# Gated layer's second projection: both column pairs by seven block products, with its token sums made in the last gated head's second group

## The chip, the cores and the metric

The kernel runs on one core of one Trainium2 chip. The metric is the device time of one execution in microseconds; the runs of the kernel before took 1377.15, 1377.93 and 1378.95 us. A core has five engines with queues of their own: TensorE (PE; its weight loads are listed as PEld), VectorE (DVE), ScalarE (ACT), GpSimd (POOL) and SyncE (SP). Each queue runs in order, and engines wait for each other by semaphores.

## The reference, cut to what matters

Two layers, one of gated linear attention and one of retention, 256 tokens, width 2048, inner width 4096, with a final norm:

```python
def gla_mixer(h, w_in, w_a1, w_a2, b_a, head_g, w_out):
    ...
    o = o * lax.rsqrt(jnp.mean(o * o, axis=-1, keepdims=True) + EPS)
    o = o.reshape(B, S, D_INNER).astype(h.dtype) * head_g
    return (o * jax.nn.silu(gate)) @ w_out

def reference(x, ...):
    h = x
    h = h + gla_mixer(rms_norm(h, gla_norm[0]), ...)
    h = h + retention_mixer(rms_norm(h, ret_norm[0]), positions, ...)
    return rms_norm(h, final_norm)
```

"Gated layer's second projection" is the last line of `gla_mixer`: a (256 x 4096) by (4096 x 2048) product. Four heads with 1024 value columns each make its left side.

## The kernel before

**Matmuls.** Every matrix is float32. A product is made of three matmuls on two-part numbers: each operand is split into a rounded part (`hi`) and a rest (`lo`), and hi·hi, hi·lo and lo·hi are summed in PSUM (`mm3`, L331; `three`, L401). Weights come in blocks of 256 contraction rows by 512 columns (512 KB). Per block, SP issues a DMA into a buffer `raw` (L252), ACT copies it to `hi` (L296), and DVE subtracts to `lo` (L297). There are four buffers of `hi` and `lo`, eight of `raw` and some spare ones; splits are emitted three blocks ahead of their use (`next_weights`, L324).

**Plain columns.** A column of 512 is 8 blocks with 12 matmuls of 128x512 each: two 128-row contraction tiles, two halves of 128 tokens, three matmuls (`steps_x`, L343).

**Pairs.** Two columns (or a value and a gate column) can be done jointly on the upper half of the contraction. There the product is 2 x 2 blocks by 2 x 2 blocks: token halves by contraction halves, contraction halves by columns. It takes seven block products instead of eight (P1, P2, P3, P5, P6, P7, P8 of 12 matmuls each, `product`, L410). The lower contraction half stays plain: blocks 4 to 7 of each column (`direct`, L417; called v4 to v7 and g4 to g7 here). The order is `UNIT`: P1 v4 P3 v5 P5 v6 P6 P2 v7 P7 g4 g5 P8 g6 g7. Sums of weight blocks are made by accumulating DMAs from POOL (L305), six per pair, and by DVE additions into `raw` (L291), two per pair. Sums of the left side over tokens and contraction halves (P3, P5, P6, P7 use them) are made once by `make_sums` (L433): two additions of 128x1024 (y), four of 128x512 (f), then four splits into `hi` and `lo` parts. The build orders instructions of an engine by itself, out of the written order, except where `keep` or a priority says otherwise; the four splits are under `keep`.

**The gated layer.** It runs in two halves of two heads each. Head h has a query/key group and two groups g = 2h, 2h+1 of value and gate. Each half ends with `out_half`: the second projection's contribution of that half's 2048 contraction rows, held transposed and split in `ogt` (16 contraction tiles; group g fills four tiles from 4(g mod 4) on). The first half's projection is called ga, the second's gb. Group 7, the second of head 3, is a pair; so is group 5. `JOINT` says which column pairs of a projection are pairs: in ga both, in gb the columns 2 and 3 only.

**What stands around gb.** `gla_head(3)` emits the last score products `o_part(1)` behind token g5 (L857); then, in steps that `advance` takes one at a time, `og_part` (L872): the norm factor `hr` (L879 to L489), the multiplications with the gate (L887), then transposes on PE (L699) and scaled splits into `ogt` (L492 on ACT, L493 on DVE). What is not yet emitted at the head's end goes on in gb (`advance`, and `drain_side` at the latest). `get_resid` loads the residual sum from DRAM by POOL (L473). `out_cols` (plain, L951) and `join` (pairs, L979) add PSUM results to it; `square_sum` (L590) and `out_transposes` (L961) prepare the next layer's left side. `slots` is the rotation of the four PSUM banks acc0 to acc3; head 0 of the retention layer takes acc0 and acc1 for two of its four query/key products, named by fixed numbers (L1263).

Of the kernel before, what the change touches and what calls it, by code (L numbers as in the profile page):

```python
# [154 lines left out]
def ret_order(h):  # L155
# [5 lines left out]
JOINT = {  # L161
    "a": (5, 7),
    ("ao", 0): (True, True),
    ("ao", 1): (False, True),
    ("ro", 0): (False, True),
    ("ro", 1): (False, False),
}
# [3 lines left out]
def kernel(  # L171
# [41 lines left out]
    def const(shape, name, dtype=F32):  # L213
        return one.tile(shape, dtype, tag=name, name=name)
# [7 lines left out]
    cur = {}  # L222
# [3 lines left out]
    def acc(n, name, shape=(P, GW), which=None):  # L226
        out = []
        for i in range(n):
            k = slots[0] if which is None else which[i]
            if which is None:  # L230
                slots.rotate(-1)
            out.append(acc_p.tile(list(shape), F32, tag=f"acc{k}", name=f"{name}{i}"))
        return out
# [75 lines left out]
    side = deque()  # L309

    def advance(n=1):
        for _ in range(n):
            while side:
                try:
                    next(side[0])
                    break
                except StopIteration:
                    side.popleft()

    def drain_side():  # L320
        while side:
            advance()
# [107 lines left out]
    def sums_in_v(name):  # L430
        return lambda n: v_p.tile([P, 2, QK, 2, P], F32R, tag="v", name=f"{name}{n}")

    def make_sums(lhs, name, where):  # L433
        s = cur["s"] = [None] * 4
        room = where(name)
        tt = nc.vector.tensor_tensor
        y = [t4_p.tile([P, QK, SEQ], F32, tag="t4", name=f"{name}_y{i}") for i in range(2)]
        for i in range(2):
            part = lhs[:, i * QK : (i + 1) * QK].bitcast(F32)
            tt(y[i], part[:, :, 0, :], part[:, :, 1, :], ALU.add)  # L440
        yield
        one_, two = slice(0, P), slice(P, SEQ)
        f = [t4_p.tile([P, 2, QK, P], F32, tag="t4", name=f"{name}_f{i}") for i in range(2)]
        f3, f5, f6, f7 = f[0][:, 0], f[0][:, 1], f[1][:, 0], f[1][:, 1]
        tt(f5, y[0][:, :, two], y[1][:, :, two], ALU.subtract)
        tt(f6, f5, y[0][:, :, one_], ALU.subtract)
        yield
        tt(f3, f6, y[1][:, :, one_], ALU.add)
        tt(f7, y[0][:, :, one_], y[0][:, :, two], ALU.subtract)
        yield  # L450
        for i, x in ((0, f3), (1, f5), (2, f6), (3, f7)):
            if i % 2 == 0:
                two_ = room(i // 2)
                s[i], s[i + 1] = two_[:, 0], two_[:, 1]
            keep(nc.scalar.activation(s[i][:, :, 0, :], x, AF.Copy))
            keep(tt(s[i][:, :, 1, :], x, s[i][:, :, 0, :].bitcast(F32), ALU.subtract))
            if i % 2:
                yield
# [42 lines left out]
    ogt = const([P, NKT, 2, SEQ], "ogt", F32R)  # L501
# [326 lines left out]
    def gla_head(h):  # L828
# [28 lines left out]
        def o_part(gi):  # L857
            g = 2 * h + gi
            if gi == 0:
                drain_side()  # L860
            po = [mis_p.tile([P, GW], F32, tag="mis", name=f"go{g}_ps{t}") for t in range(2)]
            o_mms(hw["sc"], vs[gi], po)
            o = o_p.tile([P, 2, GW], F32, tag="o", name=f"go{g}")
            with tc.high_priority():
                for t in range(2):
                    nc.scalar.activation(o[:, t, :], po[t], AF.Copy, scale=r[:, t : t + 1])
                    nc.scalar.activation(po[t], o[:, t, :], AF.Square, accum_out=sso[:, t, gi : gi + 1])
            os_.append(o)
            if gi == 1:
                side.append(og_part(0))  # L870

        def og_part(gj):  # L872
# [23 lines left out]
                f"got{g}",  # L896
            )

        def joint_turn(tok):
            if tok == "v4":  # L900
                o_part(0)
            elif tok == "g5":
                o_part(1)
            else:
                advance()

        for gi in range(2):
            g = 2 * h + gi
# [52 lines left out]
    def out_transposes(c):  # L961
        return transpose_out(
            lambda t, j: cur["resid"][:, t, c * GW + j * P : c * GW + (j + 1) * P],
            4 * c,
            S_RN + 4 * c,
            xhl,
            f"xt2_{c}",
        )

    def out_pair(c, first, name):  # L970
        lhs, s = ogt, cur["s"]
        B, A, C, V1 = acc(4, f"{name}e{c}_ps", which=list(slots))
        slots.rotate(-2)
        P5 = lev_p.tile([P, GW], F32, tag="lev", name=f"{name}e{c}_p5")
        plain = lambda kt0, t: lambda k, a: lhs[:, kt0 + k, a, t * P : (t + 1) * P]
        summed = lambda i: lambda k, a: s[i][:, k, a, :]
        u3 = t4_p.tile([P, 2, GW], F32, tag="t4", name=f"{name}e{c}_u3")[:, 0, :]

        def join(col, t, src, op=ALU.add):  # L979
            dst = cur["resid"][:, t, col * GW : (col + 1) * GW]  # L980
            if op == ALU.add:
                keep(nc.vector.tensor_tensor(dst, src, dst, ALU.add))
            else:
                keep(nc.vector.tensor_tensor(dst, dst, src, ALU.subtract))

        def whole(col, t):
            if not first:
                square_sum(t, col)

        late = deque() if first else deque([out_transposes(c)])  # L990

        def turn():
            advance()
            if late:
                next(late[0], None)

        g = c + 1
        product(A, plain(0, 0), stop=True)
        advance()
        direct(lhs, (C, V1), 4)  # L1000
        join(g, 0, A)
        advance()
        product(C, summed(0))
        advance()
        direct(lhs, (C, V1), 5)
        drain_side()
        product(P5, summed(1), stop=True)
        direct(lhs, (C, V1), 6)
        for t in range(2):
            join(c, t, P5)  # L1010
        product(A, summed(2), stop=True)
        product(B, plain(4, 0))
        join(c, 0, A, ALU.subtract)
        direct(lhs, (C, V1), 7, stop=True)
        product(A, summed(3), stop=True)
        with tc.high_priority():
            keep(nc.scalar.activation(u3, A, AF.Copy))
        join(c, 0, C)
        whole(c, 0)
        direct(lhs, (B, A), 4)  # L1020
        join(c, 1, u3, ALU.subtract)
        join(c, 1, V1)
        whole(c, 1)
        direct(lhs, (B, A), 5)
        turn()
        product(A, plain(4, 1))
        turn()
        direct(lhs, (B, A), 6)
        turn()
        direct(lhs, (B, A), 7, stop=True)  # L1030
        join(g, 0, B)
        whole(g, 0)
        join(g, 1, A)
        whole(g, 1)
        if not first:
            for _ in late[0]:
                pass
            tasks.append(out_transposes(g))
        begun.clear()
        closed.clear()  # L1040

    def out_half(first, final, name, cut=0, hook=None, joint=(False, False)):
        pend = {}
        for c in range(4):
            if joint[c // 2]:
                if c % 2 == 0:
                    out_pair(c, first, name)
                continue
            if final:
                fns[c] = gn_p.tile([P, GW], F32, tag="gn", name=f"fn{c}")  # L1050
                nc.gpsimd.dma_start(fns[c], final_norm[c * GW : (c + 1) * GW].partition_broadcast(P))
                if c == 3:
                    break
            if cut and c == 0:
                if True:
                    for i in range(2):
                        pend[i] = acc(2, f"{name}{i}_ps")
                        steps_x(pend[i], ogt, range(cut), lambda j: hook(i, j))
                    get_resid(f"{name}_resid")
                    for i in range(2):  # L1060
                        steps_x(pend[i], ogt, range(cut, NSUB), lambda j: hook(1, j))
            ps = pend[c] if c in pend else group_x(ogt, f"{name}{c}", deadline=None if c else 5)
            for t in range(2):
                out_cols(c, ps[t], t, first, final)
            if first or final:
                continue
            side.append(out_transposes(c))
            if joint[1] and c == 0:
                side.append(make_sums(ogt, "osum", sums_in_v))
# [183 lines left out]
    tasks = deque()  # L1253
# [149 lines left out]
    for h in range(2):  # L1403
        gla_head(h)
# [5 lines left out]
        gla_head(h)  # L1410
    get_resid("gb_resid")
    slots = deque((2, 3, 0, 1))
    out_half(False, False, "gb", joint=JOINT["ao", 1])
    put_resid("resid_g")
    if True:
# [119 lines left out]
```

## Time and profile before

| | us |
|---|---|
| median of three runs | 1377.93 |
| the profiled execution | 1377.54 |
| its span, first to last instruction | 1375.7 |
| head 3's group 7 | 521.1 to 566.0 |
| gb, columns 0 and 1 (plain) | 566.0 to 612.3 |
| gb, columns 2 and 3 (pair) | 612.3 to 656.0 |

How to read the rows below: a row of the timeline has the start (us from the span's start), the duration, the engine, the line of the kernel, the operation, out<-in by the program's names, and a count of equal neighbours; in brackets, idle time before it and what ended that. A grouped row has the count, the busy us, the mean ns of one and the idle time before. A row by tile has the least, median and greatest duration in ns, then the first and the last start. A row of stages has the busy us and the number of instructions of PE, PEld, DVE, ACT and POOL, then TensorE's granted clock, the DMA share and GB/s. A row of DMA issues has the count, the size and the median us to landing. A matmul's end is modelled, so a busy PE is not PE at its peak.

### The profile page before, as it was taken

How to read it: one execution, taken by the hardware profiler on the slowest of the kernel's cores; microseconds unless marked ns; L12 is line 12 of the kernel's file. 1: busy time of each engine (PE TensorE's matmuls, PEld its weight loads, DVE VectorE, ACT ScalarE, POOL GpSimd, SP SyncE). 2: the span in 40 equal slices, each digit the busy share in tenths (PEclk: the TensorE clock that was granted, in tenths of full speed). 3: DMA queues.
4: the chain of work that ended last, by engine and by line, in shares of the span. 5: the costliest groups of instructions: out<-in, count | busy, mean ns of one | idle time of the engine just before them, and what ended most of it. 6: DMA issues, size and time to landing. Idle time of an engine off the chain costs nothing.

```text
span 1375.7 us, 18380 instructions
## 1 busy us (share of the span) xinstructions
PE 1365.2 (99%) x6600; PEld 1147.2 (83%) x6600; DVE 1079.0 (78%) x1498; ACT 837.1 (61%) x1104; POOL 131.5 (10%) x188
## 2 busy tenths in 40 slices
PE   9999999999999999999999999999999999999997
PEld 7888888888888888888888888888888888888886
DVE  6686795987878896769888888886858897888672
ACT  6576656656567747656666566655546666666462
POOL 1003020110021021001011010100101101010000
PEclk9999999999999999999999999999999999999999
DMA  9755566689659667868897878896798797879751
GB/s 357 257 176 167 173 203 183 157 244 319 198 153 266 203 206 180 316 168 242 271 319 199 256 201 251 209 324 207 183 361 238 215 273 190 270 185 339 217 163 62
DMA packets 83931, 312.94 MB, mean 227 GB/s; under 512 B 9712, under 2 KB 10736, under 8 KB 82560
## 3 DMA queue, kind: packets, MB, share of 16 engines
q1 hardware_dynamic: 67488, 242.68, 51.0%
q0 software_dynamic: 15056, 61.74, 22.5%
q10 hardware_dynamic: 1296, 7.35, 1.4%
q8 instruction: 52, 0.85, 0.2%
q14 instruction: 39, 0.32, 0.1%
HBM read 301.25 MB, written 10.49 MB: 227 GB/s over the span
## 4 chain that ended last, share of the span: by engine, by line
PE 94%; DMA 3%; issue 1%; DVE 1%; ACT 1%; SPq 0%; POOL 0%; DVEq 0%; ACTq 0%; POOLq 0%
PE rqk_ps L377 8%; PE re_ps L404 8%; PE re_ps L405 8%; PE re_ps L406 8%; PE rqk_ps L378 4%; PE gqk_ps L377 4%; PE gg_ps L335 3%; PE gv_ps L336 3%; PE gv_ps L334 3%; PE gv_ps L335 3%; PE gg_ps L334 3%; PE gg_ps L336 3%; DMA raw<-in_w_all 3%; PE ge_ps L406 2%; PE ge_ps L404 2%; PE ge_ps L405 2%
## 5 line engine op out<-in xcount | busy, mean ns | idle before, releaser
L297 DVE TENSOR_TENSOR lo<-raw,hi 128x1024 fp32r<-128x1024 f32 (+1 forms) x557 | 674.7, 1221 | 220.5 <-ACT hi L296 212.7
L296 ACT ACTIVATE hi<-raw 128x1024 fp32r<-128x1024 f32 (+1 forms) x557 | 585.8, 1057 | 386.0 <-DMA raw<-in_w_all 56.5
L377 PE MATMUL rqk_ps<-xhl,hi 128*128 128x512 f32 x480 | 162.8, 397 | 0.0
L405 PE MATMUL re_ps<-lo,xhl 128*128 128x512 f32 x352 | 137.3, 390 | 0.0
L406 PE MATMUL re_ps<-hi,xhl 128*128 128x512 f32 x352 | 137.1, 390 | 0.0
L404 PE MATMUL re_ps<-hi,xhl 128*128 128x512 f32 x352 | 132.7, 391 | 0.0
L305 POOL DMA_DIRECT2D raw<-in_w_all x84 | 72.7, 867 | 531.2 <-DVE lo L297 219.5
L378 PE MATMUL rqk_ps<-xhl,lo 128*128 128x256 f32 x480 | 122.3, 280 | 0.0
L377 PEld LDWEIGHTS rqk_ps<-xhl,hi 128*128 128x128 f32 x480 | 89.5, 188 | 17.9
L378 PEld LDWEIGHTS rqk_ps<-xhl,lo 128*128 128x128 f32 x480 | 87.5, 189 | 3.4
L406 PEld LDWEIGHTS re_ps<-hi,xhl 128*128 128x128 f32 x352 | 66.1, 188 | 13.6
L404 PEld LDWEIGHTS re_ps<-hi,xhl 128*128 128x128 f32 x352 | 66.1, 188 | 13.3
L405 PEld LDWEIGHTS re_ps<-lo,xhl 128*128 128x128 f32 x352 | 66.1, 188 | 13.1
L377 PE MATMUL gqk_ps<-xhl,hi 128*128 128x512 f32 x216 | 76.6, 398 | 0.0
L335 PE MATMUL gg_ps<-lo,xhl 128*128 128x512 f32 x192 | 75.4, 393 | 0.0
L335 PE MATMUL gv_ps<-lo,xhl 128*128 128x512 f32 x192 | 75.2, 392 | 0.0
L334 PE MATMUL gv_ps<-hi,xhl 128*128 128x512 f32 x192 | 75.1, 393 | 0.0
L336 PE MATMUL gv_ps<-hi,xhl 128*128 128x512 f32 x192 | 75.0, 391 | 0.0
L336 PE MATMUL gg_ps<-hi,xhl 128*128 128x512 f32 x192 | 74.9, 390 | 0.0
L334 PE MATMUL gg_ps<-hi,xhl 128*128 128x512 f32 x192 | 74.8, 391 | 0.0
L378 PE MATMUL gqk_ps<-xhl,lo 128*128 128x256 f32 x216 | 59.0, 280 | 0.0
L821 POOL TENSOR_TENSOR s<-s,m 128x64 f32<-128x64 f32 x56 | 36.1, 677 | 232.6 <-DVE m L812 223.3
(409 smaller groups left out, 2661.9 us busy)
## 6 DMA issues: line engine op xcount, KB each, us to landing
raw<-in_w_all SPq DMA_DIRECT2D x451, 512.0 KB, 4.8
raw<-in_w_all POOLq DMA_DIRECT2D x84, 512.0 KB, 6.9
resid<-in_x_n SPq DMA_DIRECT2D x2, 1024.0 KB, 10.2
gg<-in_gn_g POOLq DMA_DIRECT2D x8, 256.0 KB, 4.3
resid_x<-resid ACTq DMA_DIRECT2D x1, 2048.0 KB, 8.1
gb<-in_gn_b POOLq DMA_DIRECT2D x8, 256.0 KB, 6.5
gb_resid<-resid_x POOLq DMA_DIRECT2D x1, 2048.0 KB, 11.0
resid_g<-gb_resid ACTq DMA_DIRECT2D x1, 2048.0 KB, 8.9
```

Of the source, the lines that this page charges most:

```text
L296: a = nc.scalar.activation(hi[:, sl], src[:, sl], AF.Copy)
L297: b = nc.vector.tensor_tensor(lo[:, sl], src[:, sl], hi[:, sl].bitcast(F32), ALU.subtract)
L305: nc.gpsimd.dma_start(raws[n], block(key), accum_op=ALU.add)
L334: mm(ps, xh, hi[:, q, :], start=kt == 0, stop=False)
L335: mm(ps, xh, lo[:, q, :], start=False, stop=False)
L336: mm(ps, xl, hi[:, q, :], start=False, stop=kt == NKT - 1)
L377: mm(ps[c], wh, rhs[:, kt, :, :], start=kt == 0, stop=False)
L378: mm(ps[c][:, 0, :], wl, rhs[:, kt, 0, :], start=False, stop=False)
L404: mm(ps, xh, hi[:, q, :], start=start, stop=False, **again)
L405: mm(ps, xh, lo[:, q, :], start=False, stop=False, **again)
L406: mm(ps, xl, hi[:, q, :], start=False, stop=stop, **again)
L821: nc.gpsimd.tensor_tensor(dst, dst, side_of(m[:, li, :], z), ALU.add)
```

## The change

Four edits. `JOINT` makes a pair of gb's columns 0 and 1. `make_sums` gets a key, and gb's token sums are made step by step behind the tokens P3, P5, P6, v7 and g6 of group 7 (which still uses the sums of the layer's input under the key "s"), not beside column 1 of gb; the call there falls away by itself, since it is in the plain branch of `out_half`. Behind head 3 the new sums take the place of the old. And the transposes of a pair's second column go to the queue `side`, which the next pair works off, when it is the first pair.

```diff
@@ JOINT
-    ("ao", 1): (False, True),
+    ("ao", 1): (True, True),
@@ make_sums
-    def make_sums(lhs, name, where):
-        s = cur["s"] = [None] * 4
+    def make_sums(lhs, name, where, key="s"):
+        s = cur[key] = [None] * 4
@@ gla_head
+        making = make_sums(ogt, "osum2", sums_in_v, "next_s") if h == 3 else None
+
         def joint_turn(tok):
+            if making and tok in ("P3", "P5", "P6", "v7", "g6"):
+                next(making)
             if tok == "v4":
                 o_part(0)
@@ out_pair
-            tasks.append(out_transposes(g))
+            (side if c == 0 else tasks).append(out_transposes(g))
@@ tile_trunk_kernel
     slots = deque((2, 3, 0, 1))
+    cur["s"] = cur["next_s"]
     out_half(False, False, "gb", joint=JOINT["ao", 1])
```

## The prediction, made before the changed kernel ran

> **What bounds the kernel now.** I read the page first, then busy time by stage, then single instructions around the changed stage.
>
> ```profile
> span 1375.7 us, 18380 instructions
> ```
> ```profile
> PE 1365.2 (99%) x6600; PEld 1147.2 (83%) x6600; DVE 1079.0 (78%) x1498; ACT 837.1 (61%) x1104; POOL 131.5 (10%) x188
> ```
> ```profile
> PE 94%; DMA 3%; issue 1%; DVE 1%; ACT 1%; SPq 0%; POOL 0%; DVEq 0%; ACTq 0%; POOLq 0%
> ```
>
> TensorE is busy for 99% of the span and is 94% of the chain that ended last, so each matmul taken away shortens the run, as long as nothing else makes TensorE wait. The stages (start:end; then length, and busy time of PE, PEld, DVE, ACT, POOL):
>
> ```profile
> 521.10:566.00 44.90, 44.90 (x200) 37.16 (x198) 34.02 (x40) 31.81 (x42) 3.98 (x5) 1.00 0.85 269
> 566.00:612.30 46.30, 46.30 (x217) 38.44 (x216) 32.23 (x44) 26.11 (x38) 1.71 (x2) 1.00 0.66 195
> 612.30:656.00 43.70, 43.70 (x202) 36.04 (x201) 40.23 (x46) 28.49 (x37) 3.47 (x4) 1.00 0.78 228
> ...
> 246.70:277.50 30.80, 30.80 (x147) 25.55 (x146) 27.05 (x32) 21.12 (x26) 4.33 (x5) 1.00 0.77 176
> ```
>
> The first is head 3's second group, g7. The second is the stage that changes: columns 0 and 1 of the second projection's second half (gb), done plainly. The third is columns 2 and 3, already a pair by seven products. The last is most of the first pair of the first half (ga), the nearest relative of the new pair. PE never idles in them, though VectorE is busy for 92% of the third and 88% of the last, against 70% of the plain stage.
>
> A matmul's printed duration overlaps the next; what counts is the step between starts:
>
> ```profile
> 566.00 0.39 PE L334 MATMUL gb_ps<-hi,ogt 128*128 128x512 f32 x1
> ...
> 569.17 0.39 PE L336 MATMUL gb_ps<-hi,ogt 128*128 128x512 f32 x1
> ```
>
> These are fifteen matmuls in a row with none between them, so 14 steps in 3.17 us: 0.2264 us each.
>
> **The change, part by part.** *Matmuls.* Two plain columns are 2 x 8 blocks x 12 = 192 matmuls of 128x512. A pair is seven products of 12 and eight direct blocks of 12, which makes 180. Twelve fewer at 0.2264 us is **-2.72 us**, the whole of the gain. Transposes are as many as before.
>
> *Weight traffic.* Sixteen block loads become fourteen on SP's queue, and six accumulating ones join POOL's.
>
> ```profile
> raw<-in_w_all SPq DMA_DIRECT2D x451, 512.0 KB, 4.8
> raw<-in_w_all POOLq DMA_DIRECT2D x84, 512.0 KB, 6.9
> ```
> ```profile
> 560.22 2.41 DVE L297 TENSOR_TENSOR lo<-raw,hi 128x1024 fp32r<-128x1024 f32 x2 [0.33 <-ACT hi L296]
> ```
> ```profile
> 551.05 0.56 POOL L473 DMA_DIRECT2D gb_resid<-resid_x  x1 [11.93 <-PE ge_ps L406]
> ```
> ```profile
> gb_resid<-resid_x POOLq DMA_DIRECT2D x1, 2048.0 KB, 11.0
> ```
>
> Fourteen pairs issue these 84 now, with PE dense in the stages above, so I cost the traffic at nothing. The residual sum is first wanted at the new pair's first join, after 24 matmuls: 566.0 + 5.4 = 571.4 us; issued at 551.05 it lands at 562, a cover of 9 us. Were it issued behind the pair's first two accumulations, which follow the splits that end at 560.22 + 2.41 = 562.6, it would land near 573.6 and hold VectorE for 2.2 us.
>
> *Weight splits and joins.* Six more splits, each an ACT copy and a DVE subtract, two raw additions and five more joins. The ga pair carries the same and keeps PE dense, so alone they cost nothing.
>
> *Token sums.* They are written in head 3's second group now, instead of beside column 1. But their large part already runs early:
>
> ```profile
> L440 DVE TENSOR_TENSOR osum_y<-ogt x4: 1208/1352/1368, 197.6 to 500.8; 128x1024 f32<-128x1024 f32 x4
> L445 DVE TENSOR_TENSOR osum_f<-osum_y,osum_y x2: 676/688/701, 200.8 to 504.9; 128x512 f32<-128x512 f32 x2
> ```
>
> The last of these additions start at 500.8 and 504.9 us, within head 3's first group: the build's ordering fills idle time with them. They stay there, at no cost. What really moves is the four splits (`keep` holds them at their written place): two behind block v7, two behind g6, 1.3 us of DVE in each couple's place by the 2.6 us row below. The first couple falls into g7, where DVE is busy for 34.0 of 44.9 us, and costs nothing; the second lands on the step that I think matters.
>
> **Where the cover is gone.** Head 3's last gated outputs are finished late, because its second group is itself a pair and its last score product comes behind block g5. A plain column wanted the contraction tiles 8 and 9 of `ogt` at its fifth block, 10.9 us in. The pair wants them in its second token, v4, 2.7 us in. P3 accumulates into the same bank behind v4, so it can't step in front. In ga the last head is plain and drains this work before the pair. The chain in gb, from ACT's last sum of squares over the multiplications to the transposes and the scaled copies (of those, a later instance):
>
> ```profile
> 562.51 0.19 ACT L867 ACTIVATION_READ_ACCUMULATOR go_ps<-go 128x1 f32 x1
> ```
> ```profile
> 562.73 0.16 DVE L879 TENSOR_TENSOR hm<-sso 128x2 f32<-128x2 f32 x1
> ...
> 565.79 0.68 DVE L1350 TENSOR_TENSOR gsg<-ge_ps,gsg 128x512 f32<-128x512 f32 x1
> ...
> 566.96 0.16 DVE L489 SCALAR_TENSOR_TENSOR hr<-hr_nw 128x2 f32<-128x2 f32 x1
> 567.16 2.08 DVE L887 SCALAR_TENSOR_TENSOR go<-go,hr,gsg 128x512 f32<-128x512 f32 x3
> ```
> ```profile
> 580.07 0.60 PE L699 MATMUL got_tp<-ident,go 128*128 128x128 f32 x4
> 580.43 0.71 PE L336 MATMUL gb_ps<-hi,ogt 128*128 128x512 f32 x2
> ```
> ```profile
> 580.71 0.47 ACT L492 ACTIVATE ogt<-got_tp,smalls 128x256 fp32r<-128x256 f32 x1 [1.60 <-PE got_tp L699]
> ```
>
> The first two of the three multiplications (L887) end at about 567.16 + 1.42 = 568.58 us. Four transposes and a scaled copy then take, by the later instance, 580.07 to 581.18 = 1.11 us, so v4 can begin at 569.69. PE gets there at 566.00 + 12 x 0.2264 + 0.36 for the transposes = 569.08. By the order of today that is a wait of **0.6 us**.
>
> What is late next is VectorE itself. Against the ga window the new pair also carries:
>
> ```profile
> L887 DVE SCALAR_TENSOR_TENSOR go<-go,hr,gsg 128x512 f32<-128x512 f32 x4 | 2.8, 748 | 0.0
> L456 DVE TENSOR_TENSOR osum<-osum_f,osum 128x512 fp32r<-128x512 f32 x4 | 2.6, 683 | 0.0
> ```
>
> That is two more multiplications (1.4 us), twelve small steps of 0.2 us (2.4, the L879 to L489 rows), the gate addition (0.7) and two sum splits (1.3): 5.8 us. On 27.05 busy of 30.80 this is 32.85 us of work, 2.05 more than the time there is, if no lead is spent. If the two sum splits also go ahead of the multiplications, v4's wait grows from 0.6 to 1.9 us. So the bounds are 0 (no gain is possible where PE is dense; the order is made anew, the multiplications go first, and the lead of the splits takes the rest) and 2.05; the two waits overlap, since VectorE works on while PE waits. I take **+1.3 us**, halfway between 0.6 and 2.0.
>
> *Handover to the retention layer.* With two pairs the bank order is turned once more: the last pair's gate columns now end in banks 0 and 1, which head 0's query/key products take next; before they ended in 2 and 3.
>
> ```profile
> 655.87 1.27 DVE L982 TENSOR_TENSOR gb_resid<-gbe_ps,gb_resid 128x512 f32<-128x512 f32 x2
> 657.28 1.22 DVE L297 TENSOR_TENSOR lo<-raw,hi 128x1024 fp32r<-128x1024 f32 x1
> ```
> ```profile
> 655.99 0.28 PE L378 MATMUL rqk_ps<-xhl,lo 128*128 128x256 f32 x1
> 656.10 0.40 PE L377 MATMUL rqk_ps<-xhl,hi 128*128 128x512 f32 x1
> ```
>
> The joins that free the banks end at about 656.5 and 657.1 us; the products that want them could begin at 656.1 at the earliest, and other products can go first. I take +0.2 us, between 0 and 1.4 (the last join's 1.0, and more if a split of 1.22 us slips ahead).
>
> **Sum.** -2.72 + 1.3 + 0.2 = -1.2 us. The profiled execution took 1377.54 us (its span 1375.7 and 1.84 around it), so 1376.3. The median of the runs, 1377.93, is 0.39 above it: **1376.7 us**.
>
> **Rivals.** *A, the cover holds:* the build's order brings the multiplications forward, and PE stays dense. For it: PE is dense in all stages quoted; against it: the 0.6 us above. 1377.93 - 2.72 = 1375.2 us. Chance 0.34.
>
> *B, slower: VectorE becomes the bound of the new pair.* Its queue is in order, and its idle time may be waits for the ACT copies that can't be filled. If it gets no more than ga's 88% of the time, 32.85 us of work takes 37.4, which is 6.6 us more than the window, so 1377.9 - 2.7 + 6.6 + 0.2 = 1382.0. It decides from the point where the splits' lead is used up, within P5 to v7. For it: 32.85 is above 30.80; against it: the gb pair lives with 92%. Chance 0.23.
>
> *C, the handover costs its whole 1.4 us* (v4's wait as forecast): 1376.7 + 1.2 = 1377.9. Chance 0.05.
>
> *D, POOL's six added issues hold VectorE off:*
>
> ```profile
> 626.56 3.65 DVE L297 TENSOR_TENSOR lo<-raw,hi 128x1024 fp32r<-128x1024 f32 x3
> ```
> ```profile
> 627.33 1.75 POOL L305 DMA_DIRECT2D raw<-in_w_all  x2 [3.07 <-DVE raw L291]
> ```
>
> Two issues ran under three splits, which took 3.65 us, no more than three times 1.22. If the added issues blocked VectorE for their 0.87 us each (half of 1.75), 5.2 us would come on top of the forecast: about 1381.9. Chance 0.02. The Trainium skill (SBUF — State Buffer, section Who interferes with whom) says that a VectorE instruction with two SBUF inputs and a GpSimd instruction that reads SBUF hold each other off entirely; by that rule D could come true, and the trace does not bear it out for these issues.
>
> **How the numbers follow.** The forecast has 0.36; its own range is 1375.2 to 1378.7, with both of its unknown terms at their low and high bounds. Faster by over 0.2% (2.76 us, below 1375.17; about what a measurement of this kernel can tell from no change) is half of A, since A lies on the bound, and the forecast's lowest part, for the runs scatter by 1.8 us (1377.15 to 1378.95): 0.22. Slower by over 0.2% (above 1380.69) is most of B and D: 0.22. The rest, 0.56, lies within. The range reaches from 1374.5, under A, to 1381.0, which leaves half of B, D and A's lowest part out, 0.2 in all.
>
> **What would show it.** The matmul lines L404 to L406 must gain 60 each, and the gb lines L334 to L336 lose their 64; L305 on POOL becomes x90, L296 and L297 x563. Right: a gap of some 0.5 to 2 us before v4's first matmuls, with ACT's scaled copy of `ogt` ending just before it, and the pair's stage at 44 to 46 us. A: no gap, and 43.6 us. B: many small waits of PE for DVE's `lo` from P5 to v7. C: a gap at the first retention products behind a join. If PE is dense and the time is not lower by 2.7 us, the matmul count or the step is wrong; if the sum additions (L440) have moved behind 521 us, my reading of the build's ordering is.

## The result, and the profile after

The changed kernel took 1382.92 us (median of six runs, 1381.91 to 1384.74); the kernel before, beside it, 1377.88 us (six runs, 1376.55 to 1378.95). The ratio is 1.0037, 95% interval 1.0027 to 1.0047: 5.0 us slower, where 1.2 us less was forecast. The profiled execution took 1384.74 us, the longest of the six, so its waits may lie at the upper end: its span is 7.0 us longer than before.

Two lines of the page: the span, and busy time by engine.

```profile
span 1382.7 us, 18396 instructions
...
PE 1366.1 (99%) x6588; PEld 1146.8 (83%) x6588; DVE 1090.4 (79%) x1511; ACT 842.4 (61%) x1111; POOL 136.6 (10%) x194
```

TensorE has 12 matmuls less, as counted, and yet is busy 0.9 us longer (1366.1 against 1365.2): some matmuls have become slower. The stages (columns as before: PE, PEld, DVE, ACT, POOL, granted clock, DMA share, GB/s) show where. They are group 7, the new pair and the second pair, parted at their first matmuls:

```profile
521.70:566.60 44.90, 44.90 (x200) 37.18 (x199) 34.84 (x39) 33.51 (x47) 5.68 (x7) 1.00 0.85 270
566.60:618.80 52.20, 46.96 (x206) 38.18 (x205) 42.54 (x58) 30.29 (x41) 5.20 (x6) 0.93 0.74 209
618.80:662.00 43.20, 43.20 (x199) 35.63 (x198) 39.91 (x45) 28.23 (x37) 3.44 (x4) 1.00 0.80 235
```

Group 7 and the second pair are dense. The new pair is not: it lasts 52.2 us where the plain columns took 46.3, PE idles for 5.2 us of it, and the granted clock is 0.93. TensorE's timeline at that place:

```profile
569.09 0.39 PE L406 MATMUL gbe_ps<-hi,ogt 128*128 128x512 f32 x1
573.83 0.44 PE L699 MATMUL got_tp<-ident,go 128*128 128x128 f32 x2 [4.36 <-DVE go L887]
575.16 1.54 PE L699 MATMUL got_tp<-ident,go 128*128 128x128 f32 x6 [0.89 <-DVE go L887]
576.62 0.80 PE L404 MATMUL gbe_ps<-hi,ogt 128*128 128x512 f32 x1
577.22 0.63 PE L405 MATMUL gbe_ps<-lo,ogt 128*128 128x512 f32 x1
...
581.06 0.66 PE L406 MATMUL gbe_ps<-hi,ogt 128*128 128x512 f32 x2
581.56 0.39 PE L404 MATMUL gbe_ps<-hi,osum 128*128 128x512 f32 x1
```

The first row is the last matmul of P1. PE then waits for VectorE's multiplications with the gate (`go`, L887), transposes, waits for the second of them, and starts v4 at 576.62. The loss, counted by starts: 573.83 - 569.09 - 0.23 = 4.5 us of waiting; 576.62 - 573.83 = 2.8 us for eight transposes and their wait, where two lots of four took 0.36 us each before, so 2.1 more; and v4's twelve matmuls from 576.62 to 581.56, 4.9 us instead of 2.7, so 2.2 more, at steps of 0.427 us instead of 0.227. Together 8.8 us, less 2.7 for the matmuls saved: 6.1 us, and the pair is 5.9 us longer than the plain columns. The last 1.1 us of the span's 7.0 stands outside the pair, in no one place. VectorE's timeline tells why `go` came so late:

```profile
564.01 1.29 DVE L456 TENSOR_TENSOR osum<-osum_f,osum 128x512 fp32r<-128x512 f32 x2
565.22 0.15 DVE L879 TENSOR_TENSOR hm<-sso 128x2 f32<-128x2 f32 x1
...
566.35 1.22 DVE L297 TENSOR_TENSOR lo<-raw,hi 128x1024 fp32r<-128x1024 f32 x1
...
568.68 1.23 DVE L297 TENSOR_TENSOR lo<-raw,hi 128x1024 fp32r<-128x1024 f32 x1
...
569.90 1.22 DVE L297 TENSOR_TENSOR lo<-raw,hi 128x1024 fp32r<-128x1024 f32 x1
...
571.10 1.22 DVE L297 TENSOR_TENSOR lo<-raw,hi 128x1024 fp32r<-128x1024 f32 x1
572.24 0.68 DVE L986 TENSOR_TENSOR gb_resid<-gbe_ps,gb_resid 128x512 f32<-128x512 f32 x1
572.84 0.15 DVE L489 SCALAR_TENSOR_TENSOR hr<-hr_nw 128x2 f32<-128x2 f32 x1
573.02 2.74 DVE L887 SCALAR_TENSOR_TENSOR go<-go,hr,gsg 128x512 f32<-128x512 f32 x4
```

From the norm's first step (`hm`) to the multiplications passed 7.8 us, where before it was 4.4 (562.73 to 567.16). The steps of the norm are 0.2 us each; between them the build put four weight splits and the pair's first join, and ahead of them the second couple of sum splits.

### The profile page after: what moved, and what is told of

It is laid out like the page before. It is cut to its first block, busy times and chain, and to the rows that moved or that the text cites. A ratio compares the mean times of both kernels' runs of the same rounds, so it can differ in the third digit from the quotient of the medians.

```text
span 1382.7 us, 18396 instructions
## 1 busy us (share of the span) xinstructions
PE 1366.1 (99%) x6588; PEld 1146.8 (83%) x6588; DVE 1090.4 (79%) x1511; ACT 842.4 (61%) x1111; POOL 136.6 (10%) x194
## 4 chain that ended last, share of the span: by engine, by line
PE 93%; DMA 3%; DVE 1%; issue 1%; ACT 1%; SPq 0%; POOL 0%; DVEq 0%; ACTq 0%; POOLq 0%
PE rqk_ps L377 8%; PE re_ps L405 8%; PE re_ps L404 8%; PE re_ps L406 8%; PE rqk_ps L378 4%; PE gqk_ps L377 4%; PE gg_ps L335 3%; PE gv_ps L335 3%; PE gv_ps L336 3%; PE gv_ps L334 3%; PE gg_ps L336 3%; PE gg_ps L334 3%; DMA raw<-in_w_all 3%; PE gbe_ps L404 2%; PE gqk_ps L378 2%; PE gbe_ps L405 2%
## 5 line engine op out<-in xcount | busy, mean ns | idle before, releaser
L297 DVE TENSOR_TENSOR lo<-raw,hi 128x1024 fp32r<-128x1024 f32 (+1 forms) x563 | 682.3, 1222 | 215.8 <-ACT hi L296 204.6
L305 POOL DMA_DIRECT2D raw<-in_w_all x90 | 77.9, 868 | 532.7 <-DVE lo L297 317.2
```

The source lines that it names most:

```text
L297: b = nc.vector.tensor_tensor(lo[:, sl], src[:, sl], hi[:, sl].bitcast(F32), ALU.subtract)
L305: nc.gpsimd.dma_start(raws[n], block(key), accum_op=ALU.add)
```

## The experiments

Theory T: what was lost is the wait of v4 for head 3's last normalization, with the slow clock behind it. Rival B: VectorE has more to do at this place than fits, so any order of the pair loses. S and K are named where they stand. All differences below are to the kernel before in the same comparison (its medians were 1377.4 to 1377.6 us, and 1377.9 beside the changed kernel). The column "0 and 1" is read from each run's trace: the time from gb's first matmul to the first of columns 2 and 3, which took 46.3 us before. Line numbers shift by one to four in the experiments.

| run | median us | to before | ratio, 95% interval | 0 and 1, us |
|---|---|---|---|---|
| changed kernel | 1382.92 | +5.0 | 1.0027 to 1.0047 | 52.2 |
| e1 sums moved, columns plain | 1379.60 | +2.1 | 1.0007 to 1.0025 | 47.9 |
| e11 additions moved alone | 1377.66 | +0.1 | 0.9995 to 1.0012 | 46.3 |
| e2 last sums later | 1381.73 | +4.2 | 1.0018 to 1.0038 | 50.5 |
| e3 v4 later | 1379.89 | +2.3 | 1.0009 to 1.0027 | 49.2 |
| e4 PE kept busy | 1381.09 | +3.5 | 1.0019 to 1.0040 | 49.7 |
| e5 v4 to v6 on other tiles | 1377.92 | +0.5 | 0.9995 to 1.0012 | 46.1 |
| e6 = e3 + e2 | 1379.64 | +2.2 | 1.0006 to 1.0024 | 48.6 |
| e7 = e6, gating on POOL | 1379.98 | +2.6 | 1.0009 to 1.0027 | 48.6 |
| e8 = e2, gating on POOL | 1380.52 | +3.1 | 1.0014 to 1.0033 | 51.0 |
| e9 = e6, weight sums on POOL | 1381.40 | +3.8 | 1.0017 to 1.0035 | 49.6 |
| e10 = e7 + e9 | 1381.35 | +3.8 | 1.0017 to 1.0037 | 52.8 |
| e12 = e6, weight sums by DMA | 1387.25 | +9.8 | 1.0055 to 1.0083 | 56.4 |
| e13 = e7, weight sums by DMA | 1389.06 | +11.6 | 1.0069 to 1.0096 | 57.3 |
| e14 = e6 without these sums | 1378.80 | +1.2 | 0.9999 to 1.0017 | 48.1 |
| e15 = e5 without these sums | 1374.98 | -2.6 | 0.9973 to 0.9990 | 44.2 |

The intervals reach 1.2 to 1.9 us to either side, so a difference of 1 us between two experiments is not clear of them by the medians alone; the last column is read beside it. It is one execution of each run, e10's the longest of its nine (1386.48 us). e5, e14 and e15 read other tiles or leave two additions out, so they do not compute the reference.

**e1 and e11: the token sums alone.** In both, columns 0 and 1 stay plain.

```diff
 e1
-    ("ao", 1): (True, True),
+    ("ao", 1): (False, True),
-            if joint[1] and c == 0:
-                side.append(make_sums(ogt, "osum", sums_in_v))
 e11, from e1
-            if making and tok in ("P3", "P5", "P6", "v7", "g6"):
+            if making and tok in ("P3", "P5", "P6"):
+            if joint[1] and c == 0:
+                side.append(cur["making"])
```

> The sums are made in head 3's second group as in the changed kernel, but columns 0 and 1 of gb keep the plain loop; nothing is left out. Theory T (the loss is v4's wait for head 3's last half, and the slow clock behind it): the plain loop reaches contraction tile 8 only 48 matmuls in, about 10.9 us (48 by 0.2264 us) behind its start, so late multiplications stay covered; about 1377.9 us, within 0.7 of before, and no gap in TensorE's row. Rival S (moving the sums' work costs TensorE time by itself): at or above 1380 us.

> e1 (plain columns 0 and 1) with only the token sums' additions left in head 3's second group; their copies and splits go back into the plain columns, behind the head's last normalization. Nothing is left out. If the additions are free and e1's 2 us are the price of copies and splits ahead of the normalization: 1377.5 us within 0.6. If the additions cost by themselves: 1379 us or more.

e1 took 2.1 us more than before, e11 0.1. So the additions cost nothing measurable when they are written in group 7 (they still run before it, from 498 us on), and the couples of copies and splits do, even where plain columns reach tile 8 only 48 matmuls in: neither S nor T's "covered" was right for e1. The multiplications on VectorE, e1 and then e11, and PE in e1:

```profile
570.30 2.73 DVE L887 SCALAR_TENSOR_TENSOR go<-go,hr,gsg 128x512 f32<-128x512 f32 x4
```
```profile
566.41 2.08 DVE L887 SCALAR_TENSOR_TENSOR go<-go,hr,gsg 128x512 f32<-128x512 f32 x3
```
```profile
576.27 0.82 PE L699 MATMUL got_tp<-ident,go 128*128 128x128 f32 x6
577.94 0.50 PE L334 MATMUL gb_ps<-hi,ogt 128*128 128x512 f32 x1 [0.85 <-ACT ogt L492]
```

Two sum splits (1.28 us) ahead of the norm put the multiplications off by 3.9 us, three times their own length: between `hm` and `go` stand three weight splits in e1 and one in e11, as before. The plain loop had, by these numbers, about 2 us of cover to spare (3.9 less 2.1).

**e2 and e8: the last couple of sums later.**

```diff
 e2
-            if making and tok in ("P3", "P5", "P6", "v7", "g6"):
+            if making and tok in ("P3", "P5", "P6", "v7"):
 out_pair, behind v5 of gb's first pair
+        if name == "gb" and c == 0:
+            next(cur["making"])
         product(P5, summed(1), stop=True)
```

> Changed kernel with one step moved: the last two sums (their copies on ScalarE, splits on VectorE) are made inside gb's first pair behind v5, ahead of P5, instead of behind the last block of head 3's second group. Nothing is left out. Theory T: that takes 2.4 us of copies and 2.6 us of splits from ahead of head 3's last normalization; the gap ahead of v4 shrinks from 4.5 us to about 2, and the slow stretch shrinks or stays; 1379 to 1381 us. If the gap falls below what the clock reacts to, 1377 to 1378. Rival B (the new pair is bound by VectorE's splits): no gain, since the same work now lies inside the pair; 1383 to 1385 us.

The expectation counted both couples; the step that moves is one, 1.14 us of copies and 1.29 of splits. The first gap shrank from 4.7 to 1.4 us, and a second wait came in its place, for the rest of the transposed output. VectorE, then PE:

```profile
568.33 2.73 DVE L887 SCALAR_TENSOR_TENSOR go<-go,hr,gsg 128x512 f32<-128x512 f32 x4
570.98 2.35 DVE L297 TENSOR_TENSOR lo<-raw,hi 128x1024 fp32r<-128x1024 f32 x2
573.25 0.68 DVE L988 TENSOR_TENSOR gb_resid<-gbe_ps,gb_resid 128x512 f32<-128x512 f32 x1
573.85 1.89 DVE L493 SCALAR_TENSOR_TENSOR ogt<-got_tp,smalls,ogt 128x256 fp32r<-128x256 f32 x4
```
```profile
574.38 1.22 PE L406 MATMUL gbe_ps<-hi,ogt 128*128 128x512 f32 x2 [1.74 <-DVE ogt L493]
```

The head's end passes VectorE twice, for `go` and for the residual of `ogt`, and each time other work stood in front. Only 0.8 us was won by the medians, 1.7 in the traces (52.2 to 50.5): short of T's range, and not the loss that B expected.

**e3 and e6: v4 24 matmuls later.**

```diff
+FIRST = "P1 P2 z P3 v4 v5 P5 v6 P6 v7 P7 g4 g5 P8 g6 g7"
 out_pair, first pair of gb
         product(A, plain(0, 0), stop=True)
+        product(B, plain(4, 0))
+        product(C, summed(0))
         advance()
         direct(lhs, (C, V1), 4)
 (and the two calls are taken out of their old places)
```

> Changed kernel with the block products of gb's first pair in the order P1, P7, P3, v4, v5, P5, v6, P6, v7, P8 instead of P1, v4, P3, v5, P5, v6, P6, P7, v7, P8; the same products, nothing left out. v4 then starts 24 matmuls (5.4 us) later, 8.2 us into the pair instead of 2.7. Theory T: the gap of 4.5 us and the slow clock behind it go, what is left is the 12 matmuls saved (2.7 us): 1375 to 1376.5 us. Rival B (the new pair is bound by VectorE whatever its order): 1380 to 1383 us.

> The order of e3 (24 matmuls more ahead of v4) together with the late sum step of e2; nothing is left out. In e3 VectorE was busy 9.47 of the 9.6 us from 566.4 to 576.0 and 9.38 of the next 10 us, with 5 us of TensorE lost in pieces. Theory T alone: with the last two sums out of the way the multiplications come 1.3 us earlier, all gaps ahead of v4 are gone, 1375 to 1376.5 us. Rival B: one pair of splits (1.29 us) and their copies (1.14 us) leave the full stretch, so about 1.3 us or a little more of e3's 1379.9 is won, 1378 to 1379 us.

Neither reached T's number. In e3 the one gap broke up into waits of three kinds, for the splits of P5, for those of P6 and for `ogt`:

```profile
576.73 0.50 PE L406 MATMUL gbe_p<-lo,osum 128*128 128x512 f32 x1 [0.63 <-DVE lo L298]
...
581.55 0.49 PE L405 MATMUL gbe_ps<-hi,osum 128*128 128x512 f32 x1 [0.63 <-ACT hi L297]
583.04 0.96 PE L407 MATMUL gbe_ps<-hi,ogt 128*128 128x512 f32 x2 [1.00 <-DVE ogt L494]
583.80 0.63 PE L405 MATMUL gbe_ps<-hi,ogt 128*128 128x512 f32 x1
```

That is B's signature. (The expectation of e3 writes P7 where the order has P2.) e6, expected by B at 1378 to 1379, won 0.1 us over e3, 0.6 in the traces: less than either said.

**e4: the clock.**

```diff
+WARM_GB = 18
         product(A, plain(0, 0), stop=True)
+        if name == "gb" and c == 0:
+            for _ in range(WARM_GB):
+                keep(mm(P5, lhs[:, 0, 0, 0:P], lhs[:, 0, :, :], start=True, stop=True))
```

> Changed kernel with 18 matmuls more (128x512, about 4.1 us) put between P1 and v4 of gb's first pair, into the bank that P5 opens anew later; their result is not used, all else is computed. Theory T (the slow steps of v4, 0.427 us instead of 0.227, follow from TensorE standing idle 4.5 us): the wait is as long as before, but v4 runs at 0.227 us; about 2.2 us less, 1380.3 to 1381.2 us. Rival K (the steps are slow for another reason, the operands or the bank): v4's steps stay at 0.43 us and the time at 1382.9 us or above.

1381.09 us, within T's range. The wait for `go` lasts as long, counted from the pair's start, but v4 runs at full speed:

```profile
568.01 4.24 PE L1006 MATMUL gbe_p<-ogt 128*128 128x512 f32 x18
572.51 0.44 PE L700 MATMUL got_tp<-ident,go 128*128 128x128 f32 x2 [0.26 <-DVE go L888]
...
574.95 0.50 PE L405 MATMUL gbe_ps<-hi,ogt 128*128 128x512 f32 x1 [0.24 <-ACT ogt L493]
575.28 0.39 PE L406 MATMUL gbe_ps<-lo,ogt 128*128 128x512 f32 x1
```

So the steps of 0.427 us follow from idling, not from operands or the bank (K). By the difference to before, 5.0 less 3.5, their share is 1.5 us, which the intervals leave open; in the traces the pair is 2.5 us shorter (52.2 to 49.7), 2.1 of it in v4's twelve matmuls (574.95 to 577.80, 2.85 us in place of 4.94).

**e5 and e15: the dependence, and what stands beside it.**

```diff
 e5, first pair of gb
-        direct(lhs, (C, V1), 4)
+        direct(lhs, (C, V1), 4, at=0)
 (v5 at=1, v6 at=2; "at" is the pair of contraction tiles that is read)
 e15, besides, and e14 from e6
                 added.add(n)
-                nc.vector.tensor_tensor(raws[at], raws[at], raws[by], ALU.add)
+                if loads[by][0][:2] != ("ao", 1) or loads[by][0][2] > 1:
+                    nc.vector.tensor_tensor(raws[at], raws[at], raws[by], ALU.add)
```

> Changed kernel, except that the direct blocks v4, v5 and v6 of gb's first pair read contraction tiles 0 to 5 in place of 8 to 13, so these three blocks no longer need head 3's last normalization; all other work, instruction by instruction, is kept. Theory T (what was lost is the dependence of the early direct blocks on head 3's end): the gap and the slow clock go and nothing comes in their place, 1375 to 1376.5 us. Rival B (VectorE has more to do in those 20 us than fits, in whatever order): the wait moves to the splits of P3 and P5 or to the transposes, 1378 to 1381 us.

> e5 (v4 to v6 on contraction tiles 0 to 5) without the same two weight additions; the output isn't the reference's. In e5 one wait of 2.10 us was left, at 589 us ahead of v7, for transposed output that VectorE got to late. Rival B: that wait goes, 1.5 to 2 us less than e5's 1377.9, the 12 matmuls show at last: 1375.5 to 1376.5 us. Theory T alone, or if what holds e5 stands behind 900 us: 1377.5 us or more.

> e6 with the two weight additions for P6 of gb's first pair left out (so P6 uses unfinished weights and the output isn't the reference's): 2.36 us of VectorE's work gone from the handover, with nothing in its place. Rival B (VectorE's load between 564 and 590 us sets the end): the waits of 0.88 and 1.81 us behind 585 us shrink by about 2 us, 1377.3 to 1378.3 us. Theory T alone (only the order of the blocks counts): as e6, 1379.6 us.

With the dependence gone and each instruction kept, 4.5 of the 5.0 us come back and the pair falls from 52.2 to 46.1 us, but the 2.7 us of the saved matmuls don't show: between T's range and B's. One wait is left in e5's pair, ahead of v7, and it is for ACT's copy of a weight block, not for the transposed output as e15's expectation has it (PE, then ACT and POOL ahead of it):

```profile
591.37 0.86 PE L404 MATMUL gbe_ps<-hi,ogt 128*128 128x512 f32 x2 [1.82 <-ACT hi L296]
```
```profile
588.96 1.06 ACT L296 ACTIVATE hi<-raw 128x1024 fp32r<-128x1024 f32 x1 [1.38 <-DMA raw<-in_w_all]
```
```profile
581.40 1.75 POOL L305 DMA_DIRECT2D raw<-in_w_all  x2 [1.54 <-DVE raw L291]
```

That copy stands behind another for which ACT waited 1.38 us until an accumulating load landed, and POOL had issued this load only when VectorE's second weight addition was done. So the path to the wait runs through the additions and the load.

With the two weight additions gone too, the kernel is 2.6 us faster than before, about what the 12 matmuls are worth (2.72), and 0.5 below B's range; the pair takes 44.2 us. Three stretches from 566.40 on (same columns), of e5 and then of e15:

```profile
566.40:576.00 9.60, 9.60 (x44) 7.93 (x44) 9.01 (x19) 6.33 (x7) 0.00 (x0) 1.00 0.74 201
576.00:586.00 10.00, 10.00 (x50) 8.29 (x49) 10.00 (x12) 6.53 (x9) 3.48 (x4) 1.00 0.56 113
586.00:596.00 10.00, 8.18 (x39) 6.32 (x38) 8.86 (x13) 5.88 (x9) 0.00 (x0) 1.00 1.05 262
```
```profile
566.40:576.00 9.60, 9.60 (x44) 7.96 (x43) 9.09 (x16) 5.62 (x6) 1.75 (x2) 1.00 1.05 246
576.00:586.00 10.00, 10.00 (x50) 8.28 (x49) 9.67 (x13) 7.70 (x10) 1.71 (x2) 1.00 0.81 166
586.00:596.00 10.00, 9.78 (x48) 7.79 (x47) 8.73 (x11) 6.58 (x10) 0.00 (x0) 1.00 1.00 358
```

VectorE is busy 10.00 of 10 us in e5's second stretch, and 9.67 in e15's. The loads differ more: POOL issues two accumulating ones in e15's first stretch and none in e5's, and the DMA share runs 1.05, 0.81, 1.00 in e15 and 0.74, 0.56, 1.05 in e5. So leaving the additions out takes 2.36 us from VectorE and also lets loads go earlier. In e5's trace the wait that is left goes by the loads; no run separates the two. Of the 2.9 us between e5 and e15 the pair has 1.9; another 0.75 us is a wait at 918 us, in the retention layer, that only e5 of the two has. In e14, where the dependence stands, the same additions were worth 1.0 us by the medians (+2.2 to +1.2) and 0.5 in the traces, between B's number and T's, and a wait of 1.32 us for `ogt` stayed.

**e7 to e10, e12 and e13: ways to carry the load elsewhere.**

```diff
 e7 (from e6) and e8 (from e2), h == 3 alone, before the norm is known
+                    nc.gpsimd.tensor_tensor(o[:, t, :], o[:, t, :], sg[:, t, :], ALU.mult)
 and in place of the four go multiplications
+                        nc.scalar.activation(o[:, t, :], o[:, t, :], AF.Copy, scale=hr[:, t : t + 1])
+                        nc.vector.tensor_scalar(o[:, t, :], o[:, t, :], hr[:, t : t + 1], None, ALU.mult)
 e9 (from e6), e10 (from e7), weight additions of gb's first pair
+                nc.gpsimd.tensor_tensor(raws[at], raws[at], raws[by], ALU.add)
 e12 (from e6), e13 (from e7): accumulating loads in their place
+                    if tok == "P5" and by_dma:
+                        post.append((x[j], (v, 2 + j)))
```

> e6 with VectorE relieved of head 3's last gating: the products of normalized-to-be output and gate are made on the idle POOL before the norm is known (four of 128x512), and the norm is applied afterwards, by two tensor_scalar of 128x512 on VectorE and two scaled copies on ScalarE, in place of VectorE's four go instructions (2.73 us together). Nothing is left out. Rival B: at least 1.4 us of VectorE's work leaves the full stretch, so 1.5 to 3 us less than e6, at or below before: 1375 to 1377 us. Theory T alone: the same as e6, unless e6 still shows a gap ahead of v4.

> The changed kernel's own order of block products, with the late sum step of e2 and the relief of e7; nothing is left out. In e2 v4's transposes waited 1.4 us for the multiplications and its third matmul 2.4 us for the second half of the transposed output, behind two splits on VectorE. Theory T: the multiplications end about 1.4 us earlier, so the first of these waits goes and the second stays; with the slow clock 1379 to 1381 us. Rival B: both shrink, 1377 to 1379 us.

> e6 with one thing more: the two additions of weight blocks for P6 of gb's first pair (raw+raw, 128x1024, 1.18 us each) are made by POOL instead of VectorE; nothing is left out. In e6 they stood at 579.5 to 581.8 us on VectorE, ahead of the residuals of the transposed output for which TensorE waited 0.88 and 1.81 us at 585 and 587. Rival B (VectorE's full stretch sets the end): these two waits shrink by about 2 us, 1377.5 to 1378.5 us. Theory T alone: as e6, 1379.6 us.

> e7 and e9 together: gate products and weight additions of the handover both on POOL; nothing is left out. Rival B: 1377 to 1378.5 us, not behind e9. If POOL's own instructions (about 1.1 us for 128x512, so some 2.2 us for 128x1024) come later than VectorE's would, P6 waits for its weights and the time is that of e6 or more.

> e6 with the two weight additions for P6 of gb's first pair (2.36 us of VectorE) made by two accumulating loads, 0.5 MB each, behind P5's splits, in place of VectorE or POOL; nothing is left out. In e9 POOL made them, and three splits on VectorE took 6.15 us meanwhile where three take 3.49 in e6, so e9 couldn't tell. Rival B (VectorE's load between 564 and 590 us sets the end): the waits of 0.88 and 1.81 us for the transposed output's residuals shrink by about 2 us, 1377.5 to 1378.5 us. Theory T alone: as e6, 1379.6 us. If the accumulating loads land too late for P6: a new wait for P6's splits, 1380 us or more.

> e12 with e7's gate products on POOL ahead of the norm; nothing is left out. Rival B: not behind e12, 1376.5 to 1378.5 us. If POOL's four products of 128x512 lengthen VectorE's instructions beside them, as in e9, nothing is won over e12.

None of them came down to the time before, and B's range was missed each time. With POOL, VectorE loses what it was to gain. In e9 (VectorE, then POOL):

```profile
581.44 6.15 DVE L299 TENSOR_TENSOR lo<-raw,hi 128x1024 fp32r<-128x1024 f32 x3 [0.41 <-ACT hi L298]
```
```profile
578.60 6.64 POOL L293 TENSOR_TENSOR raw<-raw,raw 128x1024 f32<-128x1024 f32 x2 [13.98 <-DVE lo L299]
```

POOL takes 3.3 us for an addition that VectorE makes in 1.18, and the three splits beside it take 6.15 us where e6 has

```profile
581.78 3.49 DVE L298 TENSOR_TENSOR lo<-raw,hi 128x1024 fp32r<-128x1024 f32 x3
```

In e7 a step of the norm that takes 0.16 us took 1.21 while a product ran on POOL, and a split 2.30 (VectorE, then POOL):

```profile
566.14 1.21 DVE L488 SCALAR_TENSOR_TENSOR hr_nw<-hr_nw,hm 128x2 f32<-128x2 f32 x1
...
567.69 2.30 DVE L298 TENSOR_TENSOR lo<-raw,hi 128x1024 fp32r<-128x1024 f32 x1
```
```profile
566.03 1.29 POOL L878 TENSOR_TENSOR go<-go,gsg 128x512 f32<-128x512 f32 x1 [2.30 <-ACT gsg L1376]
567.58 1.32 POOL L878 TENSOR_TENSOR go<-go,gsg 128x512 f32<-128x512 f32 x1 [0.26 <-ACT gsg L1376]
```

The Trainium skill (SBUF — State Buffer, section Who interferes with whom) says that a VectorE instruction with two inputs in SBUF and a GpSimd instruction that reads SBUF exclude each other. These rows agree: the step that began at 566.14 ended with POOL's product, at 567.35 and 567.32 us. e8's median is 1.2 us below e2's, within T's range, but its pair is no shorter (51.0 us against 50.5), and its waits fell otherwise than T said: the first grew from 1.4 to 3.2 us, and the second shrank. In e12 the accumulating loads came too late for P6's splits, the case that its expectation named last. The wait on PE's row is for `ogt`, since its copy stood behind P6's copies in ACT's queue (ACT, then PE):

```profile
586.84 1.06 ACT L300 ACTIVATE hi<-raw 128x1024 fp32r<-128x1024 f32 x1 [6.57 <-DMA raw<-in_w_all]
```
```profile
591.79 0.80 PE L408 MATMUL gbe_ps<-hi,ogt 128*128 128x512 f32 x1 [7.18 <-ACT ogt L496]
```

No form of the pair with the whole computation beat the kernel before.

## Why the prediction was wrong

- *Matmuls, -2.72 us: right.* x6588, and e15 shows 2.6 us where PE waits for no more than 0.22 us in the pair.
- *Weight traffic and residual sum, nothing: right for the changed kernel.* POOL's accumulating loads are x90, as said, no wait of TensorE in the pair goes back to a load, and the residual sum, issued at 551.6 us, landed 11.0 us later, ahead of the join at 572.24. But in e5, where the gap is gone, the wait that is left goes back to a late load.

```profile
raw<-in_w_all POOLq DMA_DIRECT2D x90, 512.0 KB, 6.9
```

- *Token sums: the additions right, the splits half right.* The additions stayed at 498 to 512 us, as read, and e11 prices them at 0.1 us. That the second couple "lands on the step that matters" was right too, but it was priced at its own 1.3 us, by which the wait would be 1.9; it put the multiplications off by 3.9 us in e1. e1 shows 2.1 us although the plain columns have 8.2 us of cover more (10.9 against 2.7).

```profile
L440 DVE TENSOR_TENSOR osum_y<-ogt x4: 1209/1352/1368, 198.2 to 501.4; 128x1024 f32<-128x1024 f32 x4
```

- *v4's wait, +1.3 us: the step that failed.* Place and cause were right: the gap stands ahead of v4, ended by `go`, its transposes and ACT's copies. The size was 8.8 us in the profiled execution, in two parts. 6.6 us is waiting. The forecast took its lower value from "today's order", in which one split stands among the norm's steps, and its upper bound, 2.05, from adding up VectorE's work over 31 us as if a surplus could spread over the whole pair. But the queue is in order and the need is early: four weight splits and a join stood between `hm` and `go`. The experiments show where they came from. There is one split with plain columns and the couple of sum splits elsewhere (before, e11), three with the couple ahead of the norm (e1), two with the pair alone (e2), four with both. So the couple brought two and the pair one, and `go` began 1.2 us (before), 5.2 (e1), 3.1 (e2) and 6.4 us (changed kernel) behind gb's first matmul. The couple is the larger part. Why the build puts the splits between the steps is not shown. The other 2.2 us is the half clock behind the wait, which had no term at all; e4 takes it away.
- *Splits and joins "alone cost nothing", by the ga pair: wrong here.* ga's pair starts behind a head that is done. In gb the same work meets the head's end; e3 and e5 show what it costs when the wait itself is moved or taken away: e5's pair takes 46.1 us where its matmuls need 43.6. The first join, too, needs only P1's 12 matmuls, not 24, and so stood ahead of `go`.
- *Handover, +0.2 us: nothing.* PE has no idle time from 616 to 880 us, so rival C is out.
- *Rivals.* A is out. B had the price (1382.0) but the wrong place, so its price was luck: it looked for small waits from P5 to v7, and in the changed kernel there is one wait ahead of v4 instead. Only when v4 moves back (e3) do B's small waits come. Rival D did not come: the splits beside the new pair's issues, from 587 to 593 us, took 1.21 to 1.22 us. For POOL's arithmetic, e7 and e9 show its mechanism.

What stays open is how the 1.9 us that e15's pair gains over e5's divide between VectorE's time and the earlier loads.

## What to carry to other kernels

Before a block is moved up in an order, look at who fills its operand and what stands in that engine's in-order queue between the last step that is late and the operand; price the wait by the new queue, not by the old one, and the added work by where it stands, not by its sum. A wait of some microseconds on TensorE has to be priced with the slow matmuls that can follow it (here 2.2 us behind 6.6). Idle time of GpSimd is not free relief for VectorE while both read SBUF.

## What was not expected of the hardware

The granted clock. Over 577 to 582 us of the changed kernel it was 0.59:

```profile
577.00:582.00 5.00, 5.00 (x14) 3.90 (x14) 1.45 (x4) 1.27 (x4) 0.00 (x0) 0.59 0.00 0
```

Behind an idle 4.36 us, 128x512 matmuls went at 0.427 us for some 5 us; behind e12's 7.18 us they did so again. A single wait of 1.82 us in e5 left the step at 0.23. But shorter waits were followed by slow steps, too: in e3 waits of 0.63 and 1.00 us with one matmul between, in e2 one of 1.01 us and two of 0.2 us with transposes between, and in e8 the one below, behind which the granted clock was 0.50 from 571.8 to 577.5 us:

```profile
570.35 1.27 PE L699 MATMUL got_tp<-ident,go 128*128 128x128 f32 x8 [2.77 <-DVE go L894]
```

The Trainium skill (TensorE: Matmul & The Clock Gate, Part 1) has half rate after an idle window of about 3.4 us, and 426.7 ns from start to start for such a matmul. The step agrees, and the two long waits agree with the window, while the waits of e2, e3 and e8 are shorter than it. What sets these apart from e5's is not settled here.
